# Down projection of a hybrid diffusion step: the low parts of the weights come from an adding transfer and not from a subtraction

## The chip, the core and the metric

The kernel runs on one core of a Trainium2 chip. Time is device time in microseconds (us), from the runs of the whole program; the profile is of one profiled execution. The engines have the names of the profile: PE multiplies matrices (PEld is its weight load), DVE is the vector engine, ACT the scalar engine, POOL is GpSimd, and SP issues most transfers.

## What is computed

One layer of a backbone for 128 context tokens and 256 latent tokens, 384 in all, with a model width of 2048. A mixing part (gated linear attention and a Fourier branch) comes first; the change lies in the feed-forward part behind it:

```python
h = rmsnorm(x, lw['norm_pre_ffn']) * (1.0 + sc2) + sh2
ff = (jax.nn.silu(h @ lw['w_ffn_gate']) * (h @ lw['w_ffn_up'])) @ lw['w_ffn_down']
x = x + ga2 * rmsnorm(ff, lw['norm_post_ffn'])
```

The hidden width is 5632. All inputs are float32.

## The kernel before

A product of two float32 matrices is made of three products of operands in the type fp32r: each operand is written as a high part (the value rounded to fp32r) and a low part (the value minus its high part), and PE adds high x high, low x high and high x low. So each granule of weights, a tile of 128 x 1024 values (512 KB), has to be split before PE can use it.

The feed-forward part cuts the hidden width into eleven chunks of 512, `c` = 0 to 10. For chunks 1 to 10 an order is written out by hand in the list `steps` (lines 1390 to 1399). A step is one granule, and its letter says what it serves. `A`, `B`, `C`, `E`, `F`, `G` and `H` belong to the gate and up projections of chunk `c`; seven combined products take the place of eight there, which is why some of these granules are sums or differences of weights that DVE makes in the buffers `u`. `D` belongs to the down projection of the chunk before. One chunk runs A0 to A3, B0 to B3, then four times C, E, D, then four times F, G, H, D. Each chunk has eight granules D, 88 in all, and the last chunk's eight stand alone at the end; the last four of these are taken up in another order by `last_products` (line 1711), token block by token block.

`grab2` (line 1487) runs once for each step: it takes the oldest granule that is split, does evictions that are due, lets SP load more (`load_more`, line 1428) and splits the next granule (`split_next`, line 1458). The buffers `whi` and `wlo` have four slots each, so the granule that is split is three places ahead of the one that PE multiplies, and its slot is that of the granule four places back. The buffer `raw` has two slots; granules of the letters R, C, G and D are loaded into it, the others lie in the eight resident slots `u` (lines 1345 to 1348, 1445). A granule D is loaded by SP from the region that `down_src` names: 128 partitions with two rows of 512 values each.

`split_next` has the high part copied by ACT (line 1467), does up to three pending evictions (`settle_pend`), makes the sums for some letters on DVE (lines 1469 to 1477), and has DVE subtract the high part from the granule (line 1478). ACT, DVE, PE and POOL run their instructions in the order of the program; SP's order is the scheduler's until the last part.

`products` (line 266) multiplies a granule D with three blocks of 128 tokens. It uses the high part first, in twelve matmuls, and the low part after it, in six. In these matmuls the weights are the moving operand, and the activations are loaded into PE. Each matmul writes 128 x 512 values into an accumulator `pdn`; after two granules it is added to the running sum in `psums` (line 1629), or, in the last chunk, by `add_last` (line 1620), which also squares it.

POOL does little: a few fills and additions in the mixing part, two subtractions of a granule at line 228, and 16 additions of the end (line 1762).

Of the kernel before, what the change touches and what calls it, by code (L numbers as in the profile page):

```python
# [11 lines left out]
F32 = mybir.dt.float32  # L12
# [3 lines left out]
ALU = mybir.AluOpType  # L16
# [5 lines left out]
D = 2048  # L22
# [74 lines left out]
def tile_step(ctx: ExitStack, tc: tile.TileContext, a, o):  # L97
    nc = tc.nc
    PE, ACT, DVE, POOL, SP = nc.tensor, nc.scalar, nc.vector, nc.gpsimd, nc.sync
# [53 lines left out]
    for h in range(2):  # L153
        for n in range(8):
            src = a["w_in"][16 + 4 * h : 20 + 4 * h, n // 4, :, 256 * (n % 4) : 256 * (n % 4) + 256]
# [26 lines left out]
    def down_src(c, n, kh):  # L182

        return a["w_d"][c, 2 * n : 2 * n + 2, :, 512 * kh : 512 * kh + 512].rearrange("i p x -> p i x")
# [455 lines left out]
    with ExitStack() as s:  # L640
# [9 lines left out]
        for c in range(2):  # L650
            src = a["a2"][:, 512 * c : 512 * c + 512]
# [224 lines left out]
    with ExitStack() as s:  # L876
# [114 lines left out]
        for h in range(2):  # L991
            p = [psm.tile([P, 512], F32, tag="mm", name="pfo") for _ in range(3)]
# [91 lines left out]
        for b, i in mix_order:  # L1084
# [9 lines left out]
            else:  # L1094
                if mT is None:
                    mT = alloc_A()
                p = psm.tile([P, T], F32, tag="mm", name="pmm")
# [16 lines left out]
    with ExitStack() as s:  # L1114
# [49 lines left out]
        for i in range(KT):  # L1164
            p = psm.tile([P, T], F32, tag="mm", name="pmm")
# [258 lines left out]
        def slot(x, c, i):  # L1424

            return 4 * ((c + x) % 2) + i
# [22 lines left out]
        def sum1(c, i):  # L1449
            x, y = (slots[slot(n, c, i)] for n in range(2))  # L1450
            DVE.tensor_sub(x, y, x)  # L1451

        def settle_pend():
            for _ in range(3):
                if pend:
                    pend.pop(0)()

        def split_next():

            if not entries:  # L1460
                settle_pend()
                return
            kind, c, i, raw = entries.pop(0)
            x, y = (slots[slot(n, c, i)] if kind not in "RD" else None for n in range(2))
            src = raw if kind in "RCGD" else y if kind == "F" else x
            hi, lo = (wp.tile([P, G], F32R, tag=t, name=t, bufs=4) for t in ("whi", "wlo"))
            ACT.copy(hi, src)  # L1467
            settle_pend()
            if (kind, i) == ("A", 3):
                sum1(c, 0)  # L1470
            elif kind == "B" and i < 3:
                sum1(c, i + 1)
            elif kind == "C":
                DVE.tensor_sub(x, raw, x)
                DVE.tensor_sub(y, raw, y)
            elif kind == "G":
                DVE.tensor_sub(x, raw, x)
            DVE.tensor_sub(lo, src, hi.bitcast(F32))  # L1478
            if kind in "RCGD":
                out_now[0] -= 1  # L1480
            elif kind == "F":
                free.add(slot(1, c, i))
            elif kind == "H":
                free.add(slot(0, c, i))
            ready.append((hi, lo))

        def grab2(kept=2):
            w = take()
            while now:
                now.pop(0)()  # L1490
            load_more(kept)
            split_next()
            return w
# [52 lines left out]
        for u in range(HEAD):  # L1546
            kind, c, j = ffn_order[u]
            dst_of[kind](hp[u], c, j)
        n = 0
        for kind, c, j in ffn_order[HEAD:]:  # L1550
            p = psm.tile([P, T], F32, tag="mm", name="pmm")
# [351 lines left out]
```

## Time and profile before

| | us |
|---|---|
| median of the two runs (1953.32 to 1954.08) | 1953.7 |
| span of the profiled execution | 1950.6 |
| PE busy | 1936.3 |
| DVE busy | 1633.1 |
| ACT busy | 906.9 |
| POOL busy | 33.6 |

The core's granted clock was 0.999 on the mean. How to read the rows in the next sections: a group of instructions has its line, engine and operation, then output<-inputs, the shapes and the count; behind the bar its busy time and the mean ns of one; behind the next bar the time for which the engine stood idle just before them, and what ended it. A row of the timeline has the start in us from the span's start, the duration, then the same names; in brackets stands the idle time before it. Rows of the same kind that follow one another are merged, with a count. "To landing" is the time from the issue of a transfer until its last byte has arrived.

### The profile page before, as it was taken

What the parts mean: (1) busy time and instruction counts of PE and PEld (TensorE: products, weight loads), DVE (VectorE), ACT (ScalarE), POOL (GpSimd) and SP (SyncE); (2) the same over time, 40 slices, a digit from 0 to 9 for tenths busy, and PEclk for the clock granted to TensorE, in tenths of its full rate; (3) what the DMA queues carried; (4) which work ended last, traced back from release to release, by engine and by line L of the source; (5) the groups of instructions that cost most, each with busy time, mean ns of one, the idle gap of its engine ahead of it and who ended that gap; (6) DMA issues with size and microseconds to landing.
All of it is one profiled execution on the core that took longest, in us unless ns stands there. A gap on an engine that the chain in (4) does not pass through costs nothing.

```text
span 1950.6 us, 27243 instructions
## 1 busy us (share of the span) xinstructions
PE 1936.3 (99%) x10422; PEld 1705.2 (87%) x10422; DVE 1633.1 (84%) x2114; ACT 906.9 (46%) x1270; POOL 33.6 (2%) x55
## 2 busy tenths in 40 slices
PE   9999999999999999999999999999999999999998
PEld 5779999999889999999988888888888888888886
DVE  5668888878777797977789898999898999887876
ACT  4233554544336654446454444444444444444444
POOL 0000000000000000004000000000000000000001
PEclk9999999999999999999999999999999999999999
DMA  9978677767765786655355535463636263626244
GB/s 391 382 255 272 228 257 239 231 218 244 239 198 178 236 265 212 233 188 210 93 157 162 172 125 179 137 199 112 199 120 209 93 216 98 211 75 194 67 157 144
DMA packets 201179, 380.12 MB, mean 195 GB/s; under 512 B 14160, under 2 KB 127508, under 8 KB 196696
## 3 DMA queue, kind: packets, MB, share of 16 engines
q1 hardware_dynamic: 200520, 378.12, 58.4%
q8 instruction: 82, 1.34, 0.3%
q14 instruction: 49, 0.40, 0.1%
q10 hardware_dynamic: 528, 0.26, 0.0%
HBM read 361.55 MB, written 16.78 MB: 194 GB/s over the span
## 4 chain that ended last, share of the span: by engine, by line
PE 96%; DVE 2%; DMA 2%; ACT 1%; issue 0%; SPq 0%; POOL 0%; DVEq 0%; ACTq 0%; POOLq 0%
PE pmm L261 32%; PE pgu L273 30%; PE pdn L273 18%; PE pfo L273 3%; PE pv L415 3%; PE pgm L398 1%; PE pf L1064 1%; PE pmm L1320 1%; DMA slab<-in_w_ada 1%; PE ptr L1612 1%; PE pf L1065 1%; PE po L673 1%; DMA xraw<-in_w_x 0%; PE px L433 0%; DMA raw<-in_w_d 0%; DVE x1b L1764 0%
## 5 line engine op out<-in xcount | busy, mean ns | idle before, releaser
L261 PE MATMUL pmm<-A_hi,whi 128*128 128x384 f32 x1072 | 361.3, 337 | 0.0
L261 PE MATMUL pmm<-A_hi,wlo 128*128 128x384 f32 x1072 | 358.6, 335 | 0.0
L261 PE MATMUL pmm<-A_lo,whi 128*128 128x384 f32 x1072 | 358.5, 334 | 0.0
L1467 ACT CAST whi<-u 128x1024 fp32r<-128x1024 f32 x200 | 210.6, 1053 | 271.0 <-DVE u L1451 86.2
L227 ACT CAST whi<-raw 128x1024 fp32r<-128x1024 f32 x181 | 189.5, 1050 | 208.1 <-DMA raw<-in_w_gate 69.0
L1467 ACT CAST whi<-raw 128x1024 fp32r<-128x1024 f32 x175 | 184.2, 1053 | 212.1 <-DMA raw<-in_w_g 68.0
L228 DVE TENSOR_TENSOR wlo<-raw,whi 128x1024 fp32r<-128x1024 f32 x179 | 218.1, 1221 | 66.2 <-ACT whi L227 65.5
L1478 DVE TENSOR_TENSOR wlo<-u,whi 128x1024 fp32r<-128x1024 f32 x200 | 243.9, 1220 | 28.1 <-ACT whi L1467 16.9
L273 PE MATMUL pgu<-whi,A_hi 128*128 128x512 f32 x640 | 250.0, 391 | 0.0
L273 PE MATMUL pgu<-whi,A_lo 128*128 128x512 f32 x640 | 249.3, 389 | 0.0
L1478 DVE TENSOR_TENSOR wlo<-raw,whi 128x1024 fp32r<-128x1024 f32 x175 | 213.3, 1219 | 33.9 <-ACT whi L1467 24.6
L600 DVE SCALAR_TENSOR_TENSOR adacc<-adaw,spad,adacc 128x1024 f32<-128x1024 f32 x180 | 222.8, 1279 | 0.3
L261 PEld LDWEIGHTS pmm<-A_hi,whi 128*128 128x128 f32 x1072 | 201.2, 188 | 3.0 <-issue 1.4
L261 PEld LDWEIGHTS pmm<-A_lo,whi 128*128 128x128 f32 x1072 | 201.3, 188 | 0.3
L261 PEld LDWEIGHTS pmm<-A_hi,wlo 128*128 128x128 f32 x1072 | 201.2, 188 | 0.0
L273 PE MATMUL pdn<-whi,hid_hi 128*128 128x512 f32 x480 | 186.9, 389 | 0.0
L273 PE MATMUL pdn<-whi,hid_lo 128*128 128x512 f32 x480 | 186.8, 389 | 0.0
L273 PE MATMUL pgu<-wlo,A_hi 128*128 128x512 f32 x640 | 184.2, 389 | 0.0
L273 PEld LDWEIGHTS pgu<-whi,A_hi 128*128 128x128 f32 x640 | 120.1, 188 | 26.0 <-issue 0.8
L273 PEld LDWEIGHTS pgu<-wlo,A_hi 128*128 128x128 f32 x640 | 120.1, 188 | 25.4
L273 PEld LDWEIGHTS pgu<-whi,A_lo 128*128 128x128 f32 x640 | 120.1, 188 | 25.0
L273 PE MATMUL pgu<-whi,S 128*128 128x512 f32 x480 | 131.1, 395 | 0.0
(386 smaller groups left out, 2900.0 us busy)
## 6 DMA issues: line engine op xcount, KB each, us to landing
adaw<-in_w_ada SPq DMA_DIRECT2D x96, 512.0 KB, 4.1
raw<-in_w_d SPq DMA_DIRECT2D x88, 512.0 KB, 4.6
slab<-in_w_ada SPq DMA_DIRECT2D x32, 1024.0 KB, 10.4
raw<-in_w_gate SPq DMA_DIRECT2D x64, 512.0 KB, 4.7
raw<-in_w_g SPq DMA_DIRECT2D x48, 512.0 KB, 4.2
raw<-in_w_u SPq DMA_DIRECT2D x48, 512.0 KB, 3.8
raw<-in_w_in SPq DMA_DIRECT2D x44, 512.0 KB, 4.2
u<-in_w_u SPq DMA_DIRECT2D x40, 512.0 KB, 4.4
```

Source lines behind the costliest of these rows:

```text
L227: ACT.copy(hi, raw)
L228: sub = lambda: eng.tensor_sub(lo, raw, hi.bitcast(F32))
L261: PE.matmul(dst, w[wi][:, k * n + n0 : k * n + n0 + P], x[xi][:, k0 + k, :], start=first and k == 0 and j == 0, stop=last and k == kts - 1 ...
L273: PE.matmul(dst, stat[x_][m], mov(w[w_], m), start=first and w_ == m == x_ == 0, stop=last and w_ == m == 1,)
L398: PE.matmul(pgv[q : q + 32, :], spad[:, k, :], slab[k // (KT // 2)][:, k % (KT // 2), :], start=k < 4, stop=k >= KT - 4,)
L415: PE.matmul(pv[2 * t + g], hT[x_][:, kb, t * P : (t + 1) * P], w_[:, g * 512 : (g + 1) * 512], start=kb == 0 and j == 0, stop=kb == KT - 1 ...
L600: DVE.scalar_tensor_tensor(acc[:, c, :], w, spad[:, k, c : c + 1], acc[:, c, :], op0=ALU.mult, op1=ALU.add,)
L673: PE.matmul(dst, w[wi], x[xi], start=first and j == 0, stop=last and j == 2)
L1064: PE.matmul(pf[:, 0 : 2 * HT], w[0][:, c], x[k], start=k == 0, stop=False)
L1065: PE.matmul(pf[:, 0:HT], w[1][:, c], x[k][:, 0:HT], start=False, stop=m == 1 and k == 3)
L1467: ACT.copy(hi, src)
L1478: DVE.tensor_sub(lo, src, hi.bitcast(F32))
```

## The change

For granules D alone, ACT also writes the low part's buffer: the high part times -1. Then a transfer issued by POOL adds the granule to it, read from DRAM a second time. DVE's subtraction is left out for these granules. The load of the granule into `raw` stays, since ACT copies the high part from there.

```diff
             ACT.copy(hi, src)
+            if kind == "D":
+                ACT.mul(lo, hi.bitcast(F32), -1.0)
+                POOL.dma_start(
+                    lo.rearrange("p (i x) -> p i x", i=2), down_src(c, i // 2, i % 2), accum_op=ALU.add,
+                )
             settle_pend()
...
-            DVE.tensor_sub(lo, src, hi.bitcast(F32))
+            if kind != "D":
+                DVE.tensor_sub(lo, src, hi.bitcast(F32))
```

`down_src`, which the new lines call, is the region that SP loads too:

```python
def down_src(c, n, kh):
    return a["w_d"][c, 2 * n : 2 * n + 2, :, 512 * kh : 512 * kh + 512].rearrange("i p x -> p i x")
```

## The prediction

> **What bounds the kernel now.** I read the page's busy shares, then its chain of work that ended last, then the windows of one chunk, then the groups by line, and last the timeline of single granules. The profiled execution spans 1950.6 us; the median of the runs is 1953.7, which is 3.1 us more (work around the span). I add my sum to the span and carry these 3.1 along.
>
> ```profile
> PE 1936.3 (99%) x10422; PEld 1705.2 (87%) x10422; DVE 1633.1 (84%) x2114; ACT 906.9 (46%) x1270; POOL 33.6 (2%) x55
> ...
> PE 96%; DVE 2%; DMA 2%; ACT 1%; issue 0%; SPq 0%; POOL 0%; DVEq 0%; ACTq 0%; POOLq 0%
> ```
>
> PE is busy for 99% of the span and is 96% of the chain. Next, the windows of one chunk: columns are the stretch, its length, then busy time (and count) of PE, PEld, DVE, ACT, POOL, then clock, DMA share and GB/s. First row: steps A and B; second: C, E, D; third: F, G, H, D.
>
> ```profile
> 1335.60:1356.50 20.90, 20.90 (x100) 17.23 (x99) 20.83 (x28) 7.87 (x10) 0.00 (x0) 1.00 0.16 51
> 1356.50:1390.00 33.50, 33.50 (x149) 27.72 (x148) 28.81 (x30) 15.58 (x17) 0.00 (x0) 1.00 0.47 141
> 1390.00:1429.70 39.70, 39.70 (x177) 32.89 (x176) 38.17 (x45) 18.95 (x19) 0.00 (x0) 1.00 0.74 238
> ```
>
> PE fills every stretch, though DVE is as full as PE in A and B. DMA share is low in A and B, and 0.74 in the F-to-D stretch. The groups by line from 1100 to 1930 us (last columns: busy us, mean ns, idle time before) show what PE waits for:
>
> ```profile
> L273 PE MATMUL pdn<-whi,hid_hi 128*128 128x512 f32 x414 | 161.2, 389 | 0.0
> L273 PE MATMUL pdn<-wlo,hid_hi 128*128 128x512 f32 x414 | 105.1, 389 | 0.0
> L1478 DVE TENSOR_TENSOR wlo<-raw,whi 128x1024 fp32r<-128x1024 f32 x144 | 175.5, 1219 | 31.6 <-ACT whi L1467 22.3 <-PE pdn L273 9.3
> L1467 ACT CAST whi<-raw 128x1024 fp32r<-128x1024 f32 x144 | 151.5, 1052 | 171.9 <-PE pgu L273 61.2 <-DMA raw<-in_w_g 43.6 <-PE pdn L273 39.6
> ```
>
> The down projection's matmuls waited 0.0 us for either part. So a cheaper DVE frees an engine on which PE does not wait: it buys nothing there, and any later low part can only cost.
>
> **The change part by part.** Removed: 88 subtractions of 1.219 us (the L1478 row), 107 us of DVE, all of it beside PE work: worth 0 in the sum.
>
> Added on ACT: 88 multiplications of a 128x1024 tile. Nearest row: the CAST at 1.05 us, so 88 x 1.05 = 92 us on an engine that is busy 46%. The multiplication also waits until PE has released the old low part in that buffer; what queues behind it on ACT are the pending evictions and the next granule's cast. The rows of the F-to-D stretch below show 1.16 to 1.72 us of idle ACT before casts, so it fits and I cost it at 0. With that cover gone it would be up to 1.05 us for each of 88.
>
> SP issues the same 88 loads of `raw` as before, since the high part still needs them, and frees each buffer earlier (after the cast and not after the subtraction): 0.
>
> Added on POOL: 88 transfers of 512 KB. POOL has no other work until the end:
>
> ```profile
> L1250 POOL TENSOR_TENSOR Clo<-t,Clo 128x384 f32<-128x384 f32 x8 | 8.1, 1021 | 2.1 <-DVE t L1246 2.1
> L1762 POOL TENSOR_TENSOR x1b<-x1b,ep 128x128 f32<-128x128 f32 x16 | 6.8, 455 | 1023.9 <-ACT ep L1761 1023.9
> L228 POOL TENSOR_TENSOR wlo<-raw,whi 128x1024 fp32r<-128x1024 f32 x2 | 4.8, 2397 | 0.0
> ```
>
> So nothing queues behind them on POOL, save the 16 additions of L1762 at the very end. The price is the chain cast, multiplication, transfer, PE. How long is the transfer, L, from the end of the multiplication to the low part's release? The trace has no DMA from POOL and none that adds. Its plain loads, by line (minimum, median, maximum to landing) and from the page:
>
> ```profile
> L1437 SPq DMA_DIRECT2D raw<-in_w_d x88: 367/368/384, 949.7 to 1914.3; - x88
> ...
> DMA to landing us min/median/max: 3.4/3.9/6.6
> ```
> ```profile
> L1445 SPq DMA_DIRECT2D u<-in_w_u x40: 367/368/584, 879.4 to 1791.8; - x40
> ...
> DMA to landing us min/median/max: 3.6/4.9/6.1
> ```
> ```profile
> L1504 SPq DMA_DIRECT2D w<-in_w_ada x64: 327/340/503, 904.8 to 1680.0; - x64
> ...
> DMA to landing us min/median/max: 2.5/2.7/4.0
> ```
> ```profile
> raw<-in_w_d SPq DMA_DIRECT2D x88, 512.0 KB, 4.6
> slab<-in_w_ada SPq DMA_DIRECT2D x32, 1024.0 KB, 10.4
> ```
>
> Low end: L = 3.4 us, the fastest 512 KB load of L1437, as if the addition were free. High end: 10.4 us, the 1 MB slab in the crowded start, plus the POOL issue. My value: an addition has to read the old content as well, so it moves a second 512 KB through the same engines. 512 KB against 256 KB costs 3.9 - 2.7 = 1.2 us, so the second 512 KB is an estimated 2.4. The issue on POOL lies between 0 and 2.4 us (the L228 row, its longest piece of work on such a tile); I take 0.7, nearer SP's 0.37. In F to D, where the `u` loads run, L = 4.9 + 2.4 + 0.7 = 8.0 us; in C to D, L = 4.6 + 2.4 + 0.7 = 7.7; high end 10.4 + 0.7 = 11.1.
>
> The Trainium skill, DMA: Bandwidth & Descriptors, section Anatomy of one DMA (SWDGE path), fits 2.0 us plus bytes over 436 GB/s, thus an estimated 4.4 us for twice 512 KB, and the total by it would be 1923.7 + 4.4 - 1924.4 = 3.7 us over, 1957. The trace speaks for longer: by that fit a plain 512 KB takes 3.2 us, and the `u` loads here take 4.9.
>
> How much time is there? Timeline rows (start, duration) for the first and the last granule D of the F-to-D stretch whose predecessor four places back is also a D (28 such):
>
> ```profile
> 1022.11 1.05 ACT L1467 CAST whi<-raw 128x1024 fp32r<-128x1024 f32 x1 [0.33 <-PE pdn L273]
> ```
> ```profile
> 1021.86 1.52 PE L273 MATMUL pdn<-wlo,hid_hi 128*128 128x512 f32 x6
> ...
> 1031.38 1.52 PE L273 MATMUL pdn<-wlo,hid_hi 128*128 128x512 f32 x6
> ```
> ```profile
> 1862.92 1.04 ACT L1467 CAST whi<-raw 128x1024 fp32r<-128x1024 f32 x1
> ...
> 1871.56 1.05 ACT L1467 CAST whi<-raw 128x1024 fp32r<-128x1024 f32 x1 [1.72 <-PE pdn L273]
> 1873.84 1.05 ACT L1467 CAST whi<-u 128x1024 fp32r<-128x1024 f32 x1 [1.23 <-PE pgu L273]
> 1876.05 1.06 ACT L1467 CAST whi<-raw 128x1024 fp32r<-128x1024 f32 x1 [1.16 <-PE pgu L273]
> ```
> ```profile
> 1871.32 1.52 PE L273 MATMUL pdn<-wlo,hid_hi 128*128 128x512 f32 x6
> ...
> 1880.84 1.52 PE L273 MATMUL pdn<-wlo,hid_hi 128*128 128x512 f32 x6
> ```
>
> The last one: its buffer for the low part is released at 1871.32 + 1.52 = 1872.84, after its cast (1872.61); the multiplication ends at 1873.9; PE wants the low part at 1880.84. That leaves 6.9 us (the first: 1031.38 - 1024.4 = 7.0). Missing at L = 8.0: 1.1 us each, 28 x 1.1 = 31 us. The granule at 1862.92 stands for the ten that come first in the stretch: cast to 1863.96, multiplication to 1865.0, used at 1871.32, so 6.3 us; missing 1.7, and 10 x 1.7 = 17 us. Together 48 us.
>
> The 40 granules of the C-to-D stretches have 5.0 to 10.0 us between cast and use, 1.1 less after the multiplication. The tightest, and the last, one of the loosest (1861.80 - 1851.76 = 10.0):
>
> ```profile
> 1264.61 1.05 ACT L1467 CAST whi<-raw 128x1024 fp32r<-128x1024 f32 x1
> ```
> ```profile
> 1270.68 1.52 PE L273 MATMUL pdn<-wlo,hid_hi 128*128 128x512 f32 x6
> ```
> ```profile
> 1850.71 1.05 ACT L1467 CAST whi<-raw 128x1024 fp32r<-128x1024 f32 x1 [0.39 <-PE pgu L273]
> ```
> ```profile
> 1861.80 1.52 PE L273 MATMUL pdn<-wlo,hid_hi 128*128 128x512 f32 x6
> ```
>
> In the tightest 1270.68 - 1265.66 - 1.1 = 3.9 us; at L = 7.7 it lacks 3.8. Taken as they stand, the 40 lack an estimated 34 us in all. I take 10: DVE's lag that makes casts late in some chunks shrinks by 8 x 1.22 = 9.8 us a chunk, and a stall at one granule gives the next one time. Both ends are kept: 0 and 34.
>
> The end: the last granule has almost no lead.
>
> ```profile
> 1921.62 1.03 ACT L1467 CAST whi<-raw 128x1024 fp32r<-128x1024 f32 x1
> ```
> ```profile
> 1922.69 1.22 DVE L1478 TENSOR_TENSOR wlo<-raw,whi 128x1024 fp32r<-128x1024 f32 x1 [2.10 <-ACT whi L1467]
> ```
> ```profile
> 1924.39 0.62 PE L273 MATMUL pdn<-wlo,hidE 128*128 128x512 f32 x2
> ```
>
> DVE finished 0.48 us ahead of use. Now: cast to 1922.65, multiplication to 1923.7, plus L = 7.7 gives 1931.4, against 1924.39: 7.0 us, with all later matmuls behind it. Sum: 48 + 10 + 7 = 65; 1950.6 + 65 = 2015.6, and with the 3.1 about 2019 us.
>
> **The rivals.** Hidden: L stays below 6.9 us (issue near SP's 0.37, second read beside the first). For it: the 3.4 us minimum; against it: the 0.74 DMA share where most granules lie. Only the end costs: at L = 6, 1923.7 + 6 - 1924.4 = 5.3, with a little from late C-to-D granules 1960 us.
>
> Not slower: DVE's relief shortens the end of the chain, where DVE has its 2%, and the last transfer lands within the 0.7 us from 1923.7 to 1924.39. It would save at most about the 1.22 us subtraction: 1953 us. Decides at L = 0.7; the 3.4 us minimum speaks against it.
>
> The transfer engines become the bound: the additions slow all transfers where the share is 0.74, or the addition itself runs slower than a copy. At L = 11.1 the F-to-D granules lack 28 x 4.2 + 10 x 4.8 = 166 us, the C-to-D ones (8.9 us at best, 2.2 short, every other one excused by its neighbour's stall) 20 x 2.2 = 44, the end 10.4: 2174 us. It decides from L = 10.
>
> DVE holds POOL back: suppose that POOL cannot set up a transfer while a two-input DVE instruction of 1.22 us runs. L grows by 1.2 to 9.2: 28 x 2.3 + 10 x 2.9 + 10 + 8 = 111, thus 2065 us. Against it: the eight L1250 additions on POOL have a mean of 1021 ns for 384 columns, and the kernel's POOL work shows no wait that ends with a long DVE instruction. The Trainium skill, SBUF — State Buffer, section Who interferes with whom, has such a lock, for DVE's two-port modes or when POOL reads SBUF; no run here shows it yet.
>
> **How the numbers follow.** Forecast (L 7 to 10, 1970 to 2110) 0.50; hidden 0.28; not slower 0.02; engines bound 0.13; POOL held back 0.07. A measurement of this kernel tells about 2% from no change, thus 1992.8 us, which is L = 7.4. Slower: 0.50 - 0.06 (L from 7.0 to 7.4) + 0.13 + 0.07 = 0.64. Faster by 2% has 0.01 of the not-slower case's 0.02, since PE has no idle time to give. Same: the rest, 0.35. The range starts at the low end of L: 1923.7 + 3.4 - 1924.4 = 2.7 us at the end alone, 1956.4, say 1957; it ends at the high end, 2174, say 2175.
>
> **What would show it.** In the profile after: `pdn<-wlo` matmuls with idle time before them, released by a DMA, mostly in F to D, and a gap of some 7 us near the last granule; DVE lower by 107 us; ACT higher by 92. A POOL transfer landing within 6.9 us makes me wrong towards 1960; one above 10 us towards 2174. Casts that wait long for `raw` would mean that the plain loads pay, which I cost at 0.

## The result, and the profile after

The changed kernel takes 2021.3 us (median of two runs, 2020.63 to 2021.89) against 1953.7: a ratio of 1.035, 95% interval 1.032 to 1.038. Its profiled execution spans 2018.8 us, 68.2 more than before. First the page after, in the order of the page before: busy time of the engines, the queues with the time of their packets as a share of 16 engines, the chain that ended last, and the transfers with their KB and median us to landing.

```profile
PE 1960.9 (97%) x10422; PEld 1712.3 (85%) x10422; DVE 1535.6 (76%) x2026; ACT 994.9 (49%) x1358; POOL 139.6 (7%) x143
...
q1 hardware_dynamic: 200520, 378.12, 56.3%
q0 software_dynamic: 23936, 46.14, 13.9%
...
PE 31%; DMA 8%; DVE 3%; issue 3%; ACT 1%; POOL 0%; DVEq 0%; ACTq 0%; POOLq 0%
...
raw<-in_w_d SPq DMA_DIRECT2D x88, 512.0 KB, 4.7
wlo<-in_w_d POOLq DMA_DIRECT2D x88, 512.0 KB, 7.1
```

DVE has lost 97.5 us of work and ACT has gained 88.0, and neither made anything faster. DMA is now 8% of the span in the chain, where it was 2%; the chain of the change is followed back only to 1052.6 us, so its shares add up to 46%. The queue q0 carries the adding transfers: 46.14 MB at 13.9%, thus 0.30% per MB, where q1's plain loads take 56.3 / 378.12 = 0.15% per MB. An added byte costs the transfer engines twice a loaded one. The window of the F-to-D stretch that the prediction showed with a DMA share of 0.74 (1390.0 to 1429.7 us) now reads, with the share before the last column:

```profile
1416.60:1459.30 42.70, 39.59 (x172) 31.60 (x171) 34.79 (x42) 22.26 (x23) 4.81 (x4) 1.00 0.97 269
```

So the transfer engines are as good as full there. Next, the groups by line that answer to the `pdn` row of before, which had 0.0 of idle time.

```profile
L273 PE MATMUL pdn<-wlo,hid_hi 128*128 128x512 f32 x480 | 129.6, 406 | 32.9 <-DMA wlo<-in_w_d 31.4 <-ACT whi L1467 1.2
L1469 ACT ACTIVATE wlo<-whi 128x1024 fp32r<-128x1024 f32 x88 | 93.4, 1061 | 40.2 <-PE pdn L273 38.2
L273 PE MATMUL pdn<-wlo,hidE 128*128 128x512 f32 x48 | 14.7, 415 | 8.1 <-DMA wlo<-in_w_d 8.1
```

PE stands still for 31.4 + 8.1 us before low parts, and a transfer ends it. Now the line of the transfers (minimum, median and maximum of the issue on POOL, and of the time to landing).

```profile
L1470 POOL DMA_DIRECT2D wlo<-in_w_d x88: 1203/1203/1335, 984.4 to 1985.1; - x88
...
  PE pdn L273: 39.5, 27
...
DMA to landing us min/median/max: 5.9/7.1/12.6
```

One granule of an F-to-D stretch, start to end:

```profile
1446.61 1.05 ACT L1467 CAST whi<-raw 128x1024 fp32r<-128x1024 f32 x1 [1.32 <-PE pdn L273]
...
1447.68 0.37 SPq L1437 DMA_DIRECT2D raw<-in_w_d  x1
1448.46 1.06 ACT L1469 ACTIVATE wlo<-whi 128x1024 fp32r<-128x1024 f32 x1 [0.81 <-PE pdn L273]
1449.82 1.20 POOL L1470 DMA_DIRECT2D wlo<-in_w_d  x1 [8.83 <-ACT wlo L1469]
1457.70 1.62 PE L273 MATMUL pdn<-wlo,hid_hi 128*128 128x512 f32 x6 [1.43 <-DMA wlo<-in_w_d]
```

The multiplication waits 0.81 us until PE lets go of the old low part and ends at 1449.52. POOL takes it up 0.30 us later, issues for 1.20, and PE goes on at 1457.70: 8.2 us after the multiplication, 1.4 too late. Two things besides the wait itself showed: at the end of the kernel the transfer engines are full, and the clock drops behind the longest waits (both below).

Where the 68.2 us went follows from the start of the first matmul of each step in both traces. At step F2 of chunk 10 these are:

```profile
1882.20 0.39 PE L273 MATMUL pgu<-whi,A_hi 128*128 128x512 f32 x1
```
```profile
1929.98 0.39 PE L273 MATMUL pgu<-whi,A_hi 128*128 128x512 f32 x1
```

So 47.8 us are lost by there, and 68.2 - 47.8 = 20.4 in the last ten granules and behind them ("end"). Of the 47.8, 2.1 are lost before the first changed granule, where the two kernels do the same (0.2 to 2.1 in the other traces); the rest is what the delay grows by across the granules named. Each row of the table stands for one profiled execution. The same reckoning for the experiments, told one by one below:

| run | C to D, 40 | F to D, first ten | F to D, other 28 | end |
|---|---|---|---|---|
| the change | 7.0 | 7.3 | 27.6 | 20.4 |
| e2: copy, no addition | 2.9 | 1.0 | 8.9 | 13.6 |
| e13: half a granule | 2.8 | 1.8 | 2.7 | 9.2 |
| e9: multiplication twice | 13.5 | 18.5 | 33.7 | 25.2 |
| e11: multiplication first | 26.1 | 22.9 | 44.1 | 22.6 |

Another 3.7 us of the change are lost in the steps behind late granules, which ran at half clock.

### The profile page after: what moved, and what is told of

Same layout as the page of the kernel before. It is cut to its first block, busy times and chain, and to the rows that moved or that the text cites. A ratio compares the mean times of both kernels' runs of the same rounds, so it can differ in the third digit from the quotient of the medians.

```text
span 2018.8 us, 27475 instructions
## 1 busy us (share of the span) xinstructions
PE 1960.9 (97%) x10422; PEld 1712.3 (85%) x10422; DVE 1535.6 (76%) x2026; ACT 994.9 (49%) x1358; POOL 139.6 (7%) x143
## 3 DMA queue, kind: packets, MB, share of 16 engines
q1 hardware_dynamic: 200520, 378.12, 56.3%
q0 software_dynamic: 23936, 46.14, 13.9%
## 5 line engine op out<-in xcount | busy, mean ns | idle before, releaser
L228 DVE TENSOR_TENSOR wlo<-raw,whi 128x1024 fp32r<-128x1024 f32 x179 | 218.3, 1222 | 67.1 <-ACT whi L227 66.5
L1470 POOL DMA_DIRECT2D wlo<-in_w_d x88 | 106.0, 1205 | 963.4 <-ACT wlo L1469 802.5
L273 PE MATMUL pdn<-wlo,hid_hi 128*128 128x512 f32 x480 | 129.6, 406 | 32.9 <-DMA wlo<-in_w_d 31.4
L273 PEld LDWEIGHTS pdn<-wlo,hid_hi 128*128 128x128 f32 x480 | 89.2, 192 | 64.2 <-issue 21.5
```

Of the source, the lines that this page charges most:

```text
L228: sub = lambda: eng.tensor_sub(lo, raw, hi.bitcast(F32))
L273: PE.matmul(dst, stat[x_][m], mov(w[w_], m), start=first and w_ == m == x_ == 0, stop=last and w_ == m == 1,)
L1470: POOL.dma_start(lo.rearrange("p (i x) -> p i x", i=2), down_src(c, i // 2, i % 2), accum_op=ALU.add,)
```

## The experiments

The theory: the change costs what the chain of multiplication, issue on POOL, and landing is longer than the time that a granule has (its budget), some 6 to 7 us; the work moved between DVE and ACT counts for nothing. Rivals: the new work on ACT or a busier transfer system costs by itself, or DVE's relief pays part of it back. Every ratio is to the kernel before on the same chip.

**e1: the multiplication alone.** The low part is only the negative high part here; the granule is not added.

```diff
                 ACT.mul(lo, hi.bitcast(F32), -1.0)
-                POOL.dma_start(...)
```

> Leaves out the transfer: the low part of the down projection's weights is only the negative high part. Theory (the low part lands too late, 46 us of stalls in the ten chunks and 20 at the end, all of it from the transfer): 1953 to 1955 us, as before. Rival 1 (the extra work on ACT delays the other casts): 1960 us or more, by up to 88 x 1.05 = 92. Rival 2 (the relief of DVE is worth something that the transfer hides): under 1951.

Measured: 1954.6 us, ratio 1.001 (1.000 to 1.002). PE's row shows what it showed before:

```profile
L273 PE MATMUL pdn<-wlo,hid_hi 128*128 128x512 f32 x480 | 121.8, 389 | 0.0
```

DVE's relief bought nothing, ACT's multiplications cost nothing, and the adding transfer is the whole loss.

**e2: copy in place of add.** The transfer writes the granule over the negative part, so the low part is the whole granule.

```diff
-    lo.rearrange(...), down_src(c, i // 2, i % 2), accum_op=ALU.add,
+    lo.rearrange(...), down_src(c, i // 2, i % 2),
```

> The transfer from POOL copies the granule over the negative high part and does not add, so the low part is the whole granule; bytes read from DRAM and POOL's issue are the same. Theory (an adding transfer costs twice the engine time because it reads the old content too): landing falls from 7.1 us by 1.2 to 2.4, the stalls in the chunks fall from 46 to under 10 us, the end from 20 to 6 to 12: 1962 to 1975 us. Rival 1 (the issue by software is the price, adding is free): landing stays at 7 us and the time at 2015 to 2023.

Measured: 1979.2 us, ratio 1.013 (1.012 to 1.015), between the two but nearer the theory. That POOL's issue would stay the same was wrong. The page's queue row, then the transfers' line:

```profile
q0 software_dynamic: 23936, 46.14, 7.7%
```
```profile
L1470 POOL DMA_DIRECT2D wlo<-in_w_d x88: 713/714/859, 984.4 to 1946.3; - x88
...
DMA to landing us min/median/max: 4.0/5.4/9.6
```

The addition costs 7.1 - 5.4 = 1.7 us of landing, 0.5 of it in the issue (1203 against 713 ns) and 1.2 in the moving. Those 1.7 us are 2021 - 1979 = 42 of the 68: most of the loss hangs on the last microseconds over the budget.

**e3 and e4: all but the last ten granules, and the last ten alone.**

```diff
-            if kind == "D":
+            by_dma = kind == "D" and 8 * c + i < 78
+            if by_dma:
...
-            if kind != "D":
+            if not by_dma:
```

In e4 the comparison is `>= 78`.

> The last ten granules of the down projection get DVE's subtraction back, the other 78 keep the transfer. Theory: the 20 us of the end go, the 46 to 48 of the chunks stay: 1998 to 2004 us. Rival (the end is late only because the earlier granules were): 2012 us or more.

> Only the last ten granules of the down projection use the transfer, the other 78 DVE's subtraction. The prediction's term for the end (one late granule, 7 us): 1961 us. Theory from the profile after (the transfer engines are full there, loads are late too, 20 us): 1970 to 1976. Rival (the end is late only because of what came before): 1955 or less.

Measured: 2000.6 us (ratio 1.026, 1.023 to 1.028) and 1975.1 (1.011, 1.010 to 1.013). Against 1953.55 that is 47.0 and 21.6, together 68.6: the two losses add up, and the end costs three times my 7.

**e8: the 40 granules of the C-to-D stretches alone** (the same edit with `i < 4 and c < NFC - 1`).

> Only the 40 granules between C, E and the next C of the ten chunks use the transfer; they have up to 8.9 us between the multiplication and PE's use. The other 48 keep DVE's subtraction. Theory (only the lead counts): 5 to 8 us of stalls, 1957 to 1964 us. Rival (the added traffic itself costs, wherever it lies): 40 of 88 parts of 67 us, 1984 us.

Measured: 1964.2 us (1.006, 1.004 to 1.008), 11.0 over 1953.1, at the upper end of the theory. The prediction's 10 for these granules, kept between 0 and 34, is borne out. With the budgets of before and the landings of the change, the 40 taken one by one lack an estimated 26.5 us, and the change lost 7.0 at them; so a late granule does give others time. How much of that is DVE's smaller lag, which the prediction also named, no run shows.

**e9: the multiplication written twice.**

```diff
                 ACT.mul(lo, hi.bitcast(F32), -1.0)
+                ACT.mul(lo, hi.bitcast(F32), -1.0)
```

> The multiplication on ACT runs twice, one after the other, ahead of each transfer; all results stay. Theory (each stall is the chain release of the slot, multiplication, transfer, use): every late granule is 1.06 us later, 38 in F to D, some of the 40 in C to D, the end: 45 to 65 us more, 2066 to 2086. Rival (the rate of the transfers sets the pace, not their latency): at most 2030 us.

Measured: 2049.4 us (1.049, 1.048 to 1.051), 28 more than the change and between the two expectations: each missed. ACT's new work costs once it stands in the chain, but less than its 1.06 us a granule:

```profile
L1471 POOL DMA_DIRECT2D wlo<-in_w_d x88: 1203/1203/1335, 983.9 to 2014.4; - x88
...
DMA to landing us min/median/max: 5.9/6.2/13.3
```

The median landing fell from 7.1 to 6.2 us. The cast frees a `raw` buffer and so lets SP issue a plain load; here POOL issues about 2 us or more behind that load (1414.33 and 1416.61 in the timeline of one granule), while in the change the distance is 0.8 to 1.4 us for 54 of the first 78. So part of the added time comes back as a quicker landing.

**e11: the multiplication ahead of the cast**, from the granule itself, so that POOL starts one cast earlier.

```diff
-            ACT.copy(hi, src)
             if kind == "D":
-                ACT.mul(lo, hi.bitcast(F32), -1.0)
+                ACT.mul(lo, src, -1.0)
                 POOL.dma_start(...)
+            ACT.copy(hi, src)
```

> For granules of the down projection ACT writes the negative part first, from the granule itself (rounded to the same value), then the high part; so the transfer can start 1.05 us earlier wherever the cast was what it waited for. Theory: the 28 granules whose slot is freed by another granule of the down projection gain nothing, since the slot's release starts their chain; the ten that come first in F to D and the 40 in C to D gain up to 1.05 each: 10 to 14 us less in the chunks, 2005 to 2013 us. Rival (all chains start with the cast): 38 x 1.05 and more, under 1985 us.

Measured: 2074.7 us (1.063, 1.061 to 1.064): 53 us slower than the change, where both expectations had it faster. One granule, then the line's landing:

```profile
1017.27 1.06 ACT L1468 ACTIVATE wlo<-raw 128x1024 fp32r<-128x1024 f32 x1 [0.39 <-PE pdn L273]
1018.23 1.03 ACT L1472 CAST whi<-raw 128x1024 fp32r<-128x1024 f32 x1
1018.63 1.20 POOL L1469 DMA_DIRECT2D wlo<-in_w_d  x1 [11.03 <-ACT wlo L1468]
1019.29 0.37 SPq L1437 DMA_DIRECT2D raw<-in_w_d  x1
```
```profile
DMA to landing us min/median/max: 6.0/8.0/11.2
```

The plain load now comes 0.66 us behind POOL's issue, a distance of under 0.8 us in 77 of the first 78 granules, and landing takes 8.0 us. A second effect: the multiplication waits for PE to release the old low part, and now the cast, and with it the next plain load, queues behind that wait. From 960 to 1930 us, ACT's waits before the multiplication and PE's before the low part are:

```profile
ACT wlo L1468 <- PE pdn L273: 117.5, 36, 5.3
...
PE pdn L273 <- DMA wlo<-in_w_d: 68.4, 53, 2.8
```

In the change they are 38.2 and 28.3 us. The runs do not part the two effects, so how much each is worth stays open.

**e13: half of each granule by transfer**, the other half by DVE as before.

```diff
-    ACT.mul(lo, hi.bitcast(F32), -1.0)
-    POOL.dma_start(...)
+    ACT.mul(lo[:, 0:512], hi[:, 0:512].bitcast(F32), -1.0)
+    POOL.dma_start(lo[:, 0:512], down_src(c, i // 2, i % 2)[:, 0, :], accum_op=ALU.add)
...
-    if kind != "D":
-        DVE.tensor_sub(lo, src, hi.bitcast(F32))
+    h0 = 512 if kind == "D" else 0
+    DVE.tensor_sub(lo[:, h0:], src[:, h0:], hi[:, h0:].bitcast(F32))
```

> The changed kernel, with the granules of the down projection split: the first 512 columns get their low part from ScalarE's negative part and an adding transfer of 256 KB, the other 512 from VectorE's subtraction as before. Theory: the loss is what a landing exceeds its budget of about 6.9 us by, and half the bytes land in 4.5 to 5.5 us: the stalls in front of the granules of the down projection come to 6 us or less in place of 46, the end loses 6 to 10 us in place of 20, in all 1960 to 1970 us. Rival: most of the landing time is a fixed price of a transfer issued by GpSimd, whatever its size, so that landing stays at 6.5 us or more: 1985 us or more.

Measured: 1970.2 us (1.009, 1.008 to 1.011), at the theory's upper end; the landing, expected at 4.5 to 5.5 us, is a little over it.

```profile
L1470 POOL DMA_DIRECT2D wlo<-in_w_d x88: 865/865/1013, 983.2 to 1937.2; - x88
...
DMA to landing us min/median/max: 3.8/5.7/8.4
```

From the multiplication's end that is 0.3 + 5.7 = 6.0 us, under the 6.9 us budget, and the losses ahead of the end shrink from 42 us to 7.3. Landing shrinks by 1.4 us for half the bytes and 0.34 less issue. The multiplication of half a granule is also shorter (0.63 us), which widens the budget. The landing against the budget decides, as argued; most of the landing time stays with half the bytes.

**e10, e12, e14, e15: what fills the end.** The windows of the change from 1925 us on, and one of before, have the stretch, busy time of PE, PEld, DVE, ACT, POOL, then clock, DMA share and GB/s:

```profile
1925.00:1950.00 25.00, 21.91 (x94) 17.83 (x93) 14.31 (x18) 13.19 (x13) 4.22 (x4) 0.95 0.71 180
1950.00:1975.00 25.00, 23.01 (x97) 18.77 (x96) 5.76 (x10) 10.07 (x12) 3.62 (x4) 0.92 0.97 264
1975.00:1990.00 15.00, 8.43 (x25) 6.01 (x24) 2.37 (x4) 10.00 (x20) 4.19 (x4) 0.77 0.99 195
```
```profile
1900.00:1925.00 25.00, 24.81 (x110) 20.21 (x109) 15.03 (x19) 13.58 (x24) 0.00 (x0) 1.00 0.50 182
```

The share is 0.97 to 0.99, where it was 0.50. A plain load issued at 1955.15 is late, a cast waits 10.7 us for it, and the last low parts are late in turn:

```profile
1971.94 1.05 ACT L1467 CAST whi<-raw 128x1024 fp32r<-128x1024 f32 x1 [10.73 <-DMA raw<-in_w_d]
```
```profile
1982.95 1.19 PE L273 MATMUL pdn<-wlo,hidE 128*128 128x512 f32 x2 [6.38 <-DMA wlo<-in_w_d]
...
1991.54 0.70 PE L273 MATMUL pdn<-wlo,hidE 128*128 128x512 f32 x2 [1.73 <-DMA wlo<-in_w_d]
```

Besides the last granules, 3.1 MB of `x1b` are loaded there, which the additions of the end need. The four runs move these loads. e10 puts them behind the last granules in the code, on SP:

```diff
-                for q in range(4):
-                    SP.dma_start(x1b[:, 4 * q : 4 * q + 4, :], x1_d[:, 4 * q : 4 * q + 4, :])
...
         last_products(0, 1)
+        for q in range(4):
+            SP.dma_start(x1b[:, 4 * q : 4 * q + 4, :], x1_d[:, 4 * q : 4 * q + 4, :])
```

> The load of x1b (3.1 MB) is issued behind the last load of the down projection's weights and not in the midst of them. Theory (the end loses 20 us since the transfer engines are full there): the 3.1 MB take some 8 us out of the stretch, 2010 to 2016 us. Rival (the end is one late granule, whatever else moves): 2019 us or more.

Measured: 2019.8 us (1.034, 1.032 to 1.036). It tells nothing: the trace has SP issue them from 1939.5 us on, among the granules as before, since SP's order is the scheduler's. By the reckoning above its end costs 18.4 us where the change's costs 20.4, with the loads among the granules in both: two executions differ by that much. e12 has ACT issue them at that place, where the order is the program's (`ACT.dma_start` in the same lines).

> The changed kernel, with the four loads of x1b (3.1 MB) issued by ScalarE behind the multiplication of the last granule of the down projection, so that they no longer share the transfer engines with the last ten granules. Theory: the end loses 20 us because the transfer engines are full there (share 0.97 to 0.99), and 3.1 MB of other loads among them take about 8 us: 2010 to 2016 us, the waits of TensorE for the last granules shorter by 5 to 11 us, the longest load of a raw granule under 12 us. Rival: the end loses what it loses by the adding transfers and their raw loads alone: 2018 us or more, with the same waits.

Measured: 2018.9 us (1.033, 1.032 to 1.035). By the total the rival is right. The trace says otherwise:

```profile
1973.68 1.03 ACT L1467 CAST whi<-raw 128x1024 fp32r<-128x1024 f32 x1
1974.75 1.06 ACT L1469 ACTIVATE wlo<-whi 128x1024 fp32r<-128x1024 f32 x1
1975.33 0.35 ACTq L1790 DMA_DIRECT2D x1b<-x_d  x1
```
```profile
1988.39 1.19 PE L273 MATMUL pdn<-wlo,hidE 128*128 128x512 f32 x2 [10.35 <-DMA wlo<-in_w_d]
```

The last cast comes at 1973.68 and not at 1982.69, since no cast waits over 4.0 us for a plain load now, where one had waited 10.7. But the 3.1 MB start just ahead of the last adding transfer, issued at 1976.1, which then takes 12.2 us. What was won at the first nine granules was lost at the tenth. So e14 puts them behind the first block's norm:

```diff
         last_products(0, 1)
+        norm(0)
         for q in range(4):
             ACT.dma_start(x1b[:, 4 * q : 4 * q + 4, :], x1_d[:, 4 * q : 4 * q + 4, :])
-        norm(0)
```

> As the run with x1b's loads behind the last multiplication, but ScalarE issues them only after the first token block's norm, when TensorE has used the last low part. Theory: in that run the four loads met the last adding transfer, which landed 12.2 us after its issue; without them it lands in about 7 us, so TensorE waits about 5 us and not 10.35 before the last granule: 2008 to 2015 us, the upper end if the loads are late for the first additions to x1b. Rival: the last transfer is late by itself, with no other load beside it: 2017 us or more, and a landing of 10 us or more.

Measured: 2015.7 us (1.031, 1.030 to 1.033), just above the expected 2015.

```profile
1985.70 1.19 PE L273 MATMUL pdn<-wlo,hidE 128*128 128x512 f32 x2 [4.35 <-DMA wlo<-in_w_d]
```

The last transfer, issued at 1979.4, lands within 6.2 us, and the wait is 4.35. e15 leaves the loads out: `POOL.memset(x1b[...], 0.0)` in their place.

> The changed kernel without the loads of x1b: GpSimd sets x1b to zero behind its last adding transfer, so the input is not added to the result, and 3.1 MB less are moved at the end. Theory: the end loses 20 us in the change, of which some 8 us are the 3.1 MB that share full transfer engines and the late plain loads that follow: 2006 to 2013 us, no landing of an adding transfer over 10.5 us and no plain load of a granule over 6 us in the last 70 us. Rival: the adding transfers and their own plain loads fill the end by themselves: 2017 us or more.

Measured: 2014.7 us (1.032, 1.029 to 1.034), above the expected 2013 (the four executions lie between 2010.4 and 2021.6), and its longest adding transfer took 11.3 us where I had said 10.5. The span less the delay up to step F2 of chunk 10 makes the totals comparable, since the runs differ by some us before it:

| run | start of F2, chunk 10 | span | end |
|---|---|---|---|
| before | 1882.2 | 1950.6 | 0 |
| the change | 1930.0 | 2018.8 | 20.4 |
| e12: x1b behind the last multiplication | 1930.0 | 2017.1 | 18.7 |
| e14: x1b behind the norm | 1932.9 | 2015.8 | 14.5 |
| e15: no x1b loads | 1926.5 | 2008.6 | 13.7 |

So some 4 to 7 of the end's 18 to 20 us (e10's 18.4 counted in) come from `x1b` sharing the engines, less than the 8 that I had expected, and some 14 from the granules' own transfers. No version beat the kernel before: its PE never waited for a low part, so there was nothing to win.

## Why the prediction held, step by step

2019 us were forecast and 2021 measured, and the mechanism is the one forecast: PE waits for adding transfers that land after its budget. The terms were less good than the sum, and that the sum came so near is in part luck: two errors of 13 us cancelled.

- **What costs nothing.** DVE's relief, ACT's multiplications and the plain loads' issue at 0: shown by e1 (1.001). The forecast DVE -107 and ACT +92 came out as -97.5 and +88.0.
- **L, forecast at 8.0 us in F to D.** From the multiplication's end to the landing it was 6.2 to 9.9 us there, 7.3 on the mean: 6.8 for the first ten, 7.5 for the other 28, of which only 17 kept PE waiting. So L was no single value. Its parts were mis-sized both ways: POOL's share is 0.30 + 1.20 and not 0.7, and the second read of the tile costs 1.2 (e2) and not 2.4. (The 3.9 us from which the 2.4 came is the median of all loads of L1437; the granules D alone take 4.6.) The Trainium skill, DMA: Bandwidth & Descriptors, section Anatomy of one DMA (SWDGE path), gave an estimated 4.4 us; the shortest of the 88 landings took 5.9, so the measurement decides against it here, for a transfer that adds.
- **F to D, forecast 48.** The other 28 lost 27.6 for 31, but the first ten 7.3 for 17: 35 in all, and 3.7 behind them. Granule by granule, what the measured L exceeds the budget of before by comes to 20 for the 28 and 5 for the ten, so the forecast's 48 was too much because L was put too high, for the first ten above all. The other 10 of the 35 lie for the greater part in the 0.14 us from a landing to the first matmul and in slower matmuls behind the waits, some at half clock (below).
- **C to D, forecast 10.** 7.0 in the change, 11.0 in e8.
- **The end, forecast 7.** It cost 20.4, and this is the step that failed: I priced the last granule's chain alone, at the L of a stretch with room. The rival in which the transfer engines become the bound came about in part: at a share of 0.97 to 0.99 the plain loads pay too, which I had at 0, one of them with 16.7 us to landing, and adding transfers take up to 12.6. In F to D the share is 0.97 as well, where it was 0.74, but L stayed below the 10 us from which that rival decides. The 13 us too little here and the 13 us too much in F to D cancelled.
- **The rivals.** Hidden is refuted by the 39.5 us of PE's waits, not slower by the interval. That DVE holds POOL back is refuted by the issue times: 1203 ns is both minimum and median of 88 issues beside a DVE that is busy 76% of the span, and the longest is 1335; POOL starts 0.30 us after the multiplication in the median, 0.97 at most.

## What to carry to other kernels

Before work is moved off an engine, look in the groups whether anyone waits for it: here PE's idle time before the low parts was 0.0, so 107 us of relief was worth 0 and only a loss was possible. Price a transfer that takes an instruction's place by its whole chain (what must be written first, the hand-over, the issue, the landing among its neighbours) against the time from that point to the use, stage by stage, and price the last stage apart, with all that is loaded there: here it cost three times what the last granule's chain alone had been priced at. And when a load is moved out of the way, ask which transfer it meets at its new place.

## What the hardware showed that I had not expected

**The clock drops behind a wait.** Two windows of the change (the last three columns are clock, DMA share and GB/s), and PE's rows around waits of different length:

```profile
1130.00:1138.40 8.40, 6.42 (x29) 4.98 (x27) 6.04 (x6) 3.48 (x4) 0.89 (x1) 1.00 1.03 285
1138.40:1141.80 3.40, 3.33 (x8) 2.69 (x9) 1.77 (x3) 0.35 (x1) 0.00 (x0) 0.50 1.09 371
```
```profile
1138.47 2.90 PE L273 MATMUL pdn<-wlo,hid_hi 128*128 128x512 f32 x6 [2.05 <-DMA wlo<-in_w_d]
...
1726.14 1.63 PE L273 MATMUL pdn<-wlo,hid_hi 128*128 128x512 f32 x6 [1.56 <-DMA wlo<-in_w_d]
```

Behind a wait of 2.05 us six matmuls take 2.90 us, and the clock is 0.50 for 3.4 us; behind 1.56 us it stays. In the chunks this happened at the four waits from 2.05 to 3.06 us and at no shorter one (the longest of those is 1.65): an estimated 4 x 1.7 = 6.8 us that no term of mine held. The length of the wait is not the whole story. The nine drops of the trace, from 1039.42 us on, lie 29, 45, 72, 120, 3, 7, 8 and 2 times 3.413 us apart, so they stand on a fixed raster. In the raster step before each of them PE had been idle for 1.86 us or more; in no other step from the first adding transfer on for more than 1.73. Behind the wait of 3.06 us, which ended at 1038.35, the drop thus came 1.07 us after PE had gone on. The Trainium skill, TensorE: Matmul & The Clock Gate, section Part 1: The HAM clock gate, has half rate after an idle window of about 3.4 us; the half rate and the 3.4 us until full speed agree, while a wait of 2.05 us was enough here.

**An adding transfer is dear in three places.** It takes 1.20 us to issue against 0.71 for a copy of the same shape by POOL, and 1.2 us more to move. Its packets take the engines 13.9% of the span for 46.14 MB, where the copy's take 7.7%.

**A neighbour's moment of issue counts.** The same adding transfer landed in a median of 6.2 us with the plain load about 2 us or more ahead of it (e9), 7.1 with it 0.8 to 1.4 us ahead (the change), and 8.0 with it 0.3 to 0.7 us behind (e11). How full the engines are does not explain the difference of e9 and e11: while these transfers were under way the share was 0.87 on the mean in both (worked out from the packets in the traces). Within the change, too, of the 28 later granules in F to D the 14 with a plain load more than 2.1 us ahead landed in 5.9 to 7.7 us, the 7 with it 1.1 to 1.4 us ahead in 8.0 to 9.6. But nine of the first ten, with the same 1.1 to 1.4 us, took 6.1 to 7.7, so the distance is not all; no run moved the load alone.
